# A hybrid attention and convolution layer on one core: the stores of precomputed input forms on ScalarE's queue, attention blocks rounded in place, and another order of copies for a paired gate

## The chip, the core and the metric

The kernel runs on one core of a Trainium2 chip. The metric is the device time of one execution in microseconds; the median of three runs before the change is 1038.19 us (1036.29 to 1043.42). TensorE is called PE in the profile, VectorE DVE, ScalarE ACT, GpSimd POOL and SyncE SP.

## The reference

256 tokens of width 2048 go through one mixer layer. All is float32.

```python
h = rmsnorm(x, pre_norm_g)
proj = h @ w_in      # q_a, c_kv, k_rope, z_mla, c_in, b_gate, c_gate, z_conv, g_mla, g_conv
q  = rmsnorm(q_a) @ w_q_b            # 16 heads, 128 plain + 64 rotary channels
kv = rmsnorm(c_kv) @ w_kv_b          # 16 heads, key 128, value 128
attn = softmax(causal(q k' * scale)) @ v
y_mla  = (attn * silu(z_mla)) @ w_o_mla
conv   = three causal taps of c_gate * c_in
y_conv = (b_gate * conv * silu(z_conv)) @ w_o_conv
merged = sigmoid(g_mla) * y_mla + sigmoid(g_conv) * y_conv
out    = x + rmsnorm(merged @ w_out, post_norm_g)
```

## The kernel before

**Products.** TensorE multiplies in a rounded float32. For full accuracy each operand is kept as a rounded part and the rest: ScalarE copies with rounding (the function split_act, its activation at L265, tile names ending in hi, or the first half of a tile such as at_both) and VectorE subtracts (L266, lo, or the second half). A product is then three matmuls. Weights come in units of 1 MB (128 x 2048), by SP into one of three buffers named raw (L167), are split in two halves of 128 x 1024 into whi and wlo (five buffers each), and a unit is 24 matmuls. TensorE takes its matmuls in the program's order, and so do the other engines their instructions; SP issues its loads in order too, each when its buffer is free.

**Stages.** From 0 to 52 us come the latents; then 16 heads follow until 600 us. A head has four quarters of channels of the convolution (cv, two accumulator banks, evicted by ScalarE or VectorE as cv_f, cv_w or cg, L807 to L824), the projections qn, kn, qr and vv, the scores (sc), a softmax and the values (o). Every four heads there are the attention's gates z. at_f and cv_f hold the branches' results. From 600 to 943 us the kernel forms the two output projections of the branches, and the two merge gates, in one interleaved list of units; then the last projection follows, to 1030 us.

**The interleaved list.** A branch block is the product of a branch with one column block of its weight, four units of 24 matmuls: p[0] to p[3] for the attention (tile at_both, bank sq), v[0] to v[3] for the convolution (cv_both). p0[3] is the fourth unit of p[0]. A set, s0 to s3, makes four gate tiles of 128 x 512 (a, b, c, d) by a scheme of seven products, Q1, V5, V6, V7, V3, V4, Q2, each two units of 12 matmuls, that multiply sums of weight blocks (rt, rb, rc, b; added on VectorE, L1272, or by an adding transfer of POOL, L1263) by sums of blocks of the input, the forms. They accumulate in the banks sX, sZ and sY. V5 and V3 write Z; V6, V7 and V4 write X. Copies from a bank are ScalarE's (L1307), sums VectorE's (L1310), and the sigmoid of a finished gate ScalarE's (L1314). interleave() puts a set's items in that order and behind each item the units named in its table; units are split two places ahead of their matmuls, and loads are sorted by when their buffer comes free and then by when they are needed. later(n, ...) puts an action n units on.

**The forms.** The generator make_forms makes the seven forms of the input long before, between the quarters of the first 14 heads, three steps a head. In four rounds SP loads two pieces of the input (x_area, L884), ScalarE scales them (L893), VectorE multiplies (L895), and for each of the seven forms ScalarE rounds into one of three buffers (form, L907), VectorE subtracts (L909, L911), and a step later SP stores 256 KB to a scratch tensor (far_form, L914), 28 stores. In the stage of the list SP loads each form whole (L937).

**The attention's blocks.** When four heads are done, POOL stores their at_f to a scratch tensor (far_at, L749, 512 KB), and SP loads it into a raw buffer (turned_at, L969), from which split_turned makes at_both. Four such pairs make the four blocks; the first two blocks are split inside the last quarter of the last head, the other two among the list's units. The channels' branch goes the same way (far_cv, L366).

Of the kernel before, what the change touches and what calls it, by code (L numbers as in the profile page):

```python
# [18 lines left out]
P = 128  # L19
# [63 lines left out]
def tile_layer(ctx: ExitStack, tc: tile.TileContext, xw, w0, xb, x, pos, pvec, post_g, wc, wz, wcv, wkr, wqk, wqr, wv, cwr, wsq, xf, out):  # L83
# [645 lines left out]
    def values(h, pt):  # L729
        vv = groups["v", h // HV]  # L730
        j = h % HV
        o = bank(f"o{h}", tag="o", bufs=1)
        vs = slice(j * DV, (j + 1) * DV)
        both = o[:, :].rearrange("p (i q) -> p i q", i=2)
        mm = matmul
        mm(both, vv[0][:, 0, vs], pt[:, :, :S], start=True, stop=False)
        yield
        mm(o[:, :S], vv[1][:, 0, vs], pt[:, 0, :S], start=False, stop=False)
        mm(o[:, P:S], vv[1][:, 1, vs], pt[:, 0, S:], start=False, stop=False)
        mm(both[:, :, P:], vv[0][:, 1, vs], pt[:, :, S:], start=False, stop=True)  # L740

        at = at_t[:, h // HV, :, :].rearrange("p t (i k x) -> p t i k x", i=4, k=HV)[:, :, :, j, :]
        f = temp("f")
        whole(f[:, :], o)
        nc.vector.tensor_tensor(at, f[:, :].rearrange("p (t i x) -> p t i x", t=NT, i=4), at, op=ALU.mult)
        if j == HV - 1:
            g = h // HV
            tc.keep_in_program_order(
                nc.gpsimd.dma_start(out=far_at[g][:, :], in_=at_f[:, 4 * g : 4 * g + 4, :].rearrange("p k s -> p (k s)"))  # L749
            )  # L750
# [3 lines left out]
    far_at, far_cv, far_m = (  # L754
        [dram.tile([P, NT * 512], F32, name=f"far_{n}{g}") for g in range(4)] for n in ("at", "cv", "m")
# [34 lines left out]
    def channels(h, i):  # L790

        if i == 0:
            cv_ps["now"] = [bank(f"cv{h}_{t}", tag="cv", bufs=2) for t in range(NT)]
        quarter(cv_ps["now"], take(u_head[h][i]), i)
        if h == H - 2 and i in (0, 2):
            u = u_first[i // 2]
            tc.keep_in_program_order(nc.sync.dma_start(out=early[u][:, :], in_=plan[u][0]))
        if i == 3:
            if h == H - 1:
                at_u[0][0]()  # L800
                ahead(u_first[0])
                for u in at_u[:2]:
                    u[1](True)
            channels_done(*divmod(h, 4))
# [71 lines left out]
    def make_forms():  # L876
# [4 lines left out]
        for c in range(KH // kq):  # L881
            for i in range(2):
# [4 lines left out]
                )  # L887
            yield
# [15 lines left out]
            def part(n, src, sign=1.0):  # L904
# [5 lines left out]
                else:  # L910
# [3 lines left out]
                    nc.sync.dma_start(  # L914
# [9 lines left out]
            for n, src, sign, following in todo:  # L924
                go = part(n, src, sign)
                if following:
                    tt(*following)
                yield
                go()
# [69 lines left out]
    at_u = [u for a, b in ((0, 2), (2, 3), (3, 4)) for u in turned_unit(far_at[a:b], at_b, a)]  # L999
    cv_u = [u for a, b in ((0, 2), (2, 4)) for u in turned_unit(far_cv[a:b], cv_b, a)]  # L1000
    for h in range(H):
# [92 lines left out]
        if h == H - 1:  # L1094
            pt = turn(ps_by_head.pop(h))
# [8 lines left out]
        if h == H - 1:  # L1104
            finish_all(values(h, pt))
        if at == 3:
# [116 lines left out]
    def weigh(nc_, t):  # L1223
# [3 lines left out]
        later(4, lambda: keep(("m", c, t), g))  # L1227
# [22 lines left out]
    def paired(i, n, c, combine):  # L1250
# [51 lines left out]
        def gate_tile(name):  # L1302
            return wide(f"s{name}{i}", "abcd"[("abcd".index(name) - i) % 4])
# [14 lines left out]
        def done_c():  # L1318
            copy("c", "X")
            later(1, lambda: plus("c", "Z"))  # L1320
            later(2, lambda: gate("c", 1, 1, -1.0))
# [9 lines left out]
        def done_y():  # L1331
# [6 lines left out]
            ("V5", (0, 0), (1, 0), (1, 1), "5", "Z", True, False, None),  # L1338
# [21 lines left out]
    def interleave(s, after):  # L1360
# [15 lines left out]
        "Q1": p[0][:2], "V5": at_u[2:3] + p[0][2:3] + at_u[3:] + p[0][3:],  # L1376
        "V6": p[1][:1], "V7": p[1][1:2], "V3": p[1][2:3], "Q2": p[1][3:] + p[2][:1],
# [291 lines left out]
```

## Time and profile before

| | us |
|---|---|
| median of 3 runs | 1038.19 |
| the profiled execution | 1039.11 |
| its span in the trace | 1037.3 |
| PE busy | 1011.0 |
| DVE busy | 806.2 |
| ACT busy | 591.8 |
| POOL busy | 171.8 |

The span is what the trace covers; the execution's own time has 1.8 us more. Busy times are shares of one span: they say which engine is full on average, while the rows of the waits say where an engine stood still and for whom. A row of the waits has the total, the number of waits and the longest; in the timeline a bracket behind a row gives the idle time before it and what ended it. A row of a chain or a timeline begins with its start and its length in us.

### The profile page before, as it was taken

Reading aid. Unit: us, or ns where it says so; the run is one execution under the profiler, and the core shown is the slowest. Engines: PE = TensorE matmul, PEld = TensorE weight load, DVE = VectorE, ACT = ScalarE, POOL = GpSimd, SP = SyncE. Lnnn points to the kernel's source line nnn. Section 1 sums busy time; section 2 is a strip of 40 time slices with the busy share of each in tenths; the row PEclk is TensorE's granted clock in tenths of the full one; section 3 lists DMA queues with packets and bytes.
Section 4 is the critical chain, followed back from the end, with each engine's and each line's share of the span. In section 5 each row is a group of like instructions: output and inputs, shape, how many; then the busy total and the mean of one; then the engine's idle time right before and its main releaser. Section 6 shows DMA issues by size and latency. Waiting matters only on the chain.

```text
span 1037.3 us, 13027 instructions
## 1 busy us (share of the span) xinstructions
PE 1011.0 (97%) x4552; PEld 836.9 (81%) x4552; DVE 806.2 (78%) x1103; ACT 591.8 (57%) x854; POOL 171.8 (17%) x315
## 2 busy tenths in 40 slices
PE   9999999999999999999999996999999999999997
PEld 8887888887888878778888875888788888878886
DVE  7589778767887677867787696889889779987562
ACT  7676656655665455555655463655665665565451
POOL 4520411203311222212133120000000101012000
PEclk9999999999999999999999998999999999999999
DMA  8775878668776688766688889697589979648842
GB/s 341 287 262 213 264 254 273 225 191 300 251 277 219 203 291 267 245 220 222 236 289 323 315 292 357 237 365 202 178 307 299 339 279 288 235 151 293 301 170 81
DMA packets 56674, 268.14 MB, mean 258 GB/s; under 512 B 9024, under 2 KB 13760, under 8 KB 31520
## 3 DMA queue, kind: packets, MB, share of 16 engines
q1 hardware_dynamic: 43488, 225.89, 59.9%
q0 software_dynamic: 12832, 40.23, 14.3%
q10 hardware_dynamic: 288, 1.20, 0.3%
q8 instruction: 35, 0.57, 0.2%
q14 instruction: 31, 0.25, 0.1%
HBM read 238.99 MB, written 24.12 MB: 254 GB/s over the span
## 4 chain that ended last, share of the span: by engine, by line
PE 88%; DMA 7%; DVE 3%; ACT 1%; issue 1%; SPq 0%; DVEq 0%; ACTq 0%
PE cv L88 28%; PE sq L88 16%; PE sX L88 8%; PE out L88 8%; PE z L88 8%; DMA far_form<-form 4%; PE sZ L88 4%; PE qa L88 2%; PE sY L88 2%; PE ckv L88 2%; PE vv L88 2%; PE kn L88 2%; PE qn L88 2%; DMA raw<-wsq_dram 1%; DVE wlo L266 1%; DMA x_area<-xf_dram 1%
## 5 line engine op out<-in xcount | busy, mean ns | idle before, releaser
L265 ACT ACTIVATE whi<-raw 128x1024 fp32r<-128x1024 f32 (+1 forms) x302 | 305.3, 1027 | 234.6 <-PE cv L88 89.4
L266 DVE TENSOR_TENSOR wlo<-raw,whi 128x1024 fp32r<-128x1024 f32 (+1 forms) x300 | 352.4, 1189 | 108.9 <-ACT whi L265 81.8
L88 PE MATMUL cv<-whi,x_both 128*128 128x512 f32 x1024 | 321.0, 390 | 4.7 <-ACT cv_f L811 2.9
L88 PEld LDWEIGHTS cv<-whi,x_both 128*128 128x128 f32 x1024 | 192.2, 188 | 46.1 <-ACT cv_f L811 3.7
L88 PE MATMUL cv<-wlo,x_both 128*128 128x512 f32 x512 | 199.6, 390 | 0.9 <-DVE wlo L266 0.9
L88 PEld LDWEIGHTS cv<-wlo,x_both 128*128 128x128 f32 x512 | 96.1, 188 | 20.3 <-DVE wlo L266 1.2
L266 DVE TENSOR_TENSOR slo_V<-b,shi_V 128x1024 fp32r<-128x1024 f32 x60 | 71.8, 1222 | 18.7 <-PE sq L88 12.1
L265 ACT ACTIVATE shi_V<-b 128x1024 fp32r<-128x1024 f32 x60 | 61.5, 1053 | 39.8 <-PE sq L88 22.7
L88 PE MATMUL z<-whi,x_both 128*128 128x512 f32 x256 | 79.9, 389 | 0.0
L366 POOL DMA_DIRECT2D far<-via x64 | 35.2, 557 | 227.1 <-DVE via L358 224.7
L88 PE MATMUL sq<-whi,at_both 128*128 128x512 f32 x256 | 63.4, 402 | 5.6 <-ACT whi L265 5.6
L88 PEld LDWEIGHTS sq<-whi,at_both 128*128 128x128 f32 x256 | 49.9, 195 | 16.7 <-ACT whi L265 6.0
L88 PE MATMUL sq<-whi,cv_both 128*128 128x512 f32 x256 | 60.6, 389 | 0.0
L88 PEld LDWEIGHTS sq<-whi,cv_both 128*128 128x128 f32 x256 | 48.0, 188 | 10.0
L88 PEld LDWEIGHTS z<-whi,x_both 128*128 128x128 f32 x256 | 48.1, 188 | 9.9
L88 PE MATMUL z<-wlo,x_both 128*128 128x512 f32 x128 | 49.8, 389 | 0.0
L88 PE MATMUL out<-whi,m_both 128*128 128x512 f32 x208 | 49.4, 389 | 0.0
L88 PE MATMUL sX<-shi_V,form 128*128 128x512 f32 x192 | 47.4, 389 | 0.0
L88 PEld LDWEIGHTS out<-whi,m_both 128*128 128x128 f32 x208 | 39.0, 188 | 8.1
L88 PEld LDWEIGHTS sX<-shi_V,form 128*128 128x128 f32 x192 | 36.0, 188 | 7.5
L1263 POOL DMA_DIRECT2D b<-wsq_dram x8 | 6.9, 863 | 208.6 <-DVE b L1272 95.7
L265 ACT ACTIVATE shi_Q<-b 128x1024 fp32r<-128x1024 f32 x28 | 28.8, 1052 | 22.1 <-PE sq L88 17.7
(305 smaller groups left out, 1572.7 us busy)
## 6 DMA issues: line engine op xcount, KB each, us to landing
raw<-wcv_dram SPq DMA_DIRECT2D x64, 1024.0 KB, 6.3
raw<-wsq_dram SPq DMA_DIRECT2D x48, 1024.0 KB, 6.9
b<-wsq_dram SPq DMA_DIRECT2D x26, 1024.0 KB, 5.1
raw<-wz_dram SPq DMA_DIRECT2D x16, 1024.0 KB, 4.9
raw<-wqk_dram SPq DMA_DIRECT2D x8, 1024.0 KB, 7.6
b<-wsq_dram POOLq DMA_DIRECT2D x8, 1024.0 KB, 9.2
far_form<-form SPq DMA_DIRECT2D x28, 256.0 KB, 7.5
form<-far_form SPq DMA_DIRECT2D x7, 1024.0 KB, 10.9
```

What stands on the lines that cost most here:

```text
L88: return tc.keep_in_program_order(nc.tensor.matmul(*a, **kw))
L265: a = nc.scalar.activation(hi, src, AF.Copy)
L266: b = nc.vector.tensor_tensor(lo, src, hi.bitcast(F32), op=ALU.subtract)
L366: tc.keep_in_program_order(queue.dma_start(out=f[i], in_=m))
L1263: tc.keep_in_program_order(nc.gpsimd.dma_start(out=dst[:, :], in_=wsq[n, c + b, k], accum_op=ALU.add))
```

## The change

It has four edits.

- The forms' stores are issued by ScalarE instead of SP. Loading a round's input becomes a function, bring(c): the first is called ahead of the rounds with a step of its own, the next when the last form of a round is made, so that every round's scaling falls a step later than it did.
- The attention blocks are split from at_f, where they lie, by split_branch(i): blocks 0 and 1 before the last head's pt, block 2 in its last quarter, block 3 behind its values. far_at, turned_at and their four stores and four loads are gone. The first branch unit is loaded and split before the last values.
- In s0's table all four units of p[0] stand behind Q1, and the units of p[1] move to V5, V6, V7 and Q2.
- Of gate c, which is the sum of banks Z and X, ScalarE copies Z one unit after V5, VectorE adds X right behind V7, and the sigmoid comes a unit later; before, ScalarE copied X behind V7, VectorE added Z a unit later, and the sigmoid came after two. The gate tiles' tags rotate in another order, and the weighed tiles are stored two units later instead of four.

```diff
@@ -743,16 +743,11 @@
         nc.vector.tensor_tensor(at, f[:, :].rearrange("p (t i x) -> p t i x", t=NT, i=4), at, op=ALU.mult)
-        if j == HV - 1:
-            g = h // HV
-            tc.keep_in_program_order(
-                nc.gpsimd.dma_start(out=far_at[g][:, :], in_=at_f[:, 4 * g : 4 * g + 4, :].rearrange("p k s -> p (k s)"))
-            )
...
     at_t = at_f[:, :, :].rearrange("p (v t k) s -> p v t (k s)", v=NV, t=NT)
-    far_at, far_cv, far_m = (
-        [dram.tile([P, NT * 512], F32, name=f"far_{n}{g}") for g in range(4)] for n in ("at", "cv", "m")
+    far_cv, far_m = (
+        [dram.tile([P, NT * 512], F32, name=f"far_{n}{g}") for g in range(4)] for n in ("cv", "m")
     )
@@ -797,10 +792,8 @@
             if h == H - 1:
-                at_u[0][0]()
                 ahead(u_first[0])
-                for u in at_u[:2]:
-                    u[1](True)
+                split_branch(2)
             channels_done(*divmod(h, 4))
@@ -878,13 +871,17 @@
         sums_2 = [early_pool.tile([P, kq, P], F32, name=f"form_sum{i}") for i in range(2)]
-        for c in range(KH // kq):
+        def bring(c):
             for i in range(2):
...
                 )
+
+        bring(0)
+        yield
+        for c in range(KH // kq):
             yield
@@ -911,7 +908,7 @@
                 return lambda: tc.keep_in_program_order(
-                    nc.sync.dma_start(
+                    nc.scalar.dma_start(
                         out=far_form[n][:, c * w : (c + 1) * w], in_=f[:, :, :, :].rearrange("p k j c -> p (k j c)").bitcast(F32)
@@ -925,6 +922,8 @@
                     tt(*following)
+                if n == "3" and c < KH // kq - 1:
+                    bring(c + 1)
                 yield
@@ -996,7 +995,11 @@
     at_b, cv_b = (Late(n, lambda i, n=n: both_tile(n, i)) for n in ("at", "cv"))
-    at_u = [u for a, b in ((0, 2), (2, 3), (3, 4)) for u in turned_unit(far_at[a:b], at_b, a)]
+
+    def split_branch(i):
+        for t in range(NT):
+            split_turned(at_t[:, i, t, :], at_b[i], t, True)
+
     cv_u = [u for a, b in ((0, 2), (2, 4)) for u in turned_unit(far_cv[a:b], cv_b, a)]
@@ -1092,6 +1095,8 @@
         if h == H - 1:
+            split_branch(0)
+            split_branch(1)
             pt = turn(ps_by_head.pop(h))
@@ -1102,7 +1107,11 @@
         if h == H - 1:
+            load_raw(done["raw"])
+            split_unit(done["split"])
+            done.update(raw=done["raw"] + 1, split=done["split"] + 1)
             finish_all(values(h, pt))
+            split_branch(3)
         if at == 3:
@@ -1224,7 +1233,7 @@
         nc.vector.tensor_tensor(g[:, :], sums_of[n, c][t][:, :], g[:, :], op=ALU.mult)
-        later(4, lambda: keep(("m", c, t), g))
+        later(2, lambda: keep(("m", c, t), g))
@@ -1300,7 +1309,10 @@
         def gate_tile(name):
-            return wide(f"s{name}{i}", "abcd"[("abcd".index(name) - i) % 4])
+            tags = list("acbd")
+            for _ in range(i):
+                tags = tags[3:] + tags[:3]
+            return wide(f"s{name}{i}", tags["acbd".index(name)])
@@ -1316,9 +1328,8 @@
         def done_c():
-            copy("c", "X")
-            later(1, lambda: plus("c", "Z"))
-            later(2, lambda: gate("c", 1, 1, -1.0))
+            plus("c", "X")
+            later(1, lambda: gate("c", 1, 1, -1.0))
@@ -1335,7 +1346,7 @@
             ("Q1", (0, 0), None, None, "11", "X", True, False, lambda: copy("a", "X")),
-            ("V5", (0, 0), (1, 0), (1, 1), "5", "Z", True, False, None),
+            ("V5", (0, 0), (1, 0), (1, 1), "5", "Z", True, False, lambda: later(1, lambda: copy("c", "Z"))),
             ("V6", (0, 0), (1, 2), (0, 0) if by_transfer else None, "6", "X", False, False, lambda: copy("b", "X")),
@@ -1373,8 +1384,7 @@
     interleave(s0, {
-        "Q1": p[0][:2], "V5": at_u[2:3] + p[0][2:3] + at_u[3:] + p[0][3:],
-        "V6": p[1][:1], "V7": p[1][1:2], "V3": p[1][2:3], "Q2": p[1][3:] + p[2][:1],
+        "Q1": p[0], "V5": p[1][:1], "V6": p[1][1:2], "V7": p[1][2:3], "Q2": p[1][3:] + p[2][:1],
     })
```

Three places show how the instructions move. The first is ScalarE in a round of forms, at about 375 to 387 us of the trace before; a form's number ends in its tile, whi is a weight's rounding. Before:

```order
L907 ACTIVATE form_2_3874<-form_sum_1014 128x2x128
L265 ACTIVATE whi_0_3680<-raw_3643 128x1024
L265 ACTIVATE whi_1024_3684<-raw_3643 128x1024
L265 ACTIVATE whi_0_3732<-raw_3678 128x1024
L265 ACTIVATE whi_1024_3736<-raw_3678 128x1024
L265 ACTIVATE whi_0_3798<-raw_3730 128x1024
L433 ACTIVATE half<-qr_3688 128x256
L907 ACTIVATE form_2_3913<-form_sum_1015 128x2x128
L811 ACTIVATE cv_f<-cv_0_3547,r_both 128x512
```

And now:

```order
L911 DMA far_form_653<-form_2_3629 128x512
L904 ACTIVATE form_2_3820<-form_sum_1010 128x2x128
L904 ACTIVATE form_2_3863<-form_sum_1011 128x2x128
L265 ACTIVATE whi_0_3669<-raw_3632 128x1024
L265 ACTIVATE whi_1024_3673<-raw_3632 128x1024
L265 ACTIVATE whi_0_3721<-raw_3667 128x1024
L265 ACTIVATE whi_1024_3725<-raw_3667 128x1024
L265 ACTIVATE whi_0_3787<-raw_3719 128x1024
L433 ACTIVATE half<-qr_3677 128x256
L804 ACTIVATE cv_f<-cv_0_3538,r_both 128x512
```

The rounding of the second form has moved from the row before the cv_f eviction to the start of the run of weight roundings, and the store of a form that used the same set of three buffers stands ahead of the two roundings.

The second place is SP at the transition from the heads to the list, at about 606 to 633 us; raw_5943 is p0[3] and raw_5966 p1[0] before, raw_5743 to raw_5827 are p0[0] to p0[3] now, and raw_5852 is p1[0]. Before:

```order
L1258 DMA first_rc_5787<-wsq_dram 128x2048
L1258 DMA first_rc_5788<-wsq_dram 128x2048
L167 DMA raw_5828<-wsq_dram 128x2048
L969 DMA turned_at_5852<-far_at_643 128x1024
L937 DMA form_5789<-far_form_655 128x2048
L167 DMA raw_5943<-wsq_dram 128x2048
L937 DMA form_5790<-far_form_656 128x2048
L167 DMA raw_5966<-wsq_dram 128x2048
```

And now:

```order
L167 DMA raw_5743<-wsq_dram 128x2048
L167 DMA raw_5805<-wsq_dram 128x2048
L167 DMA raw_5807<-wsq_dram 128x2048
L1267 DMA first_rb_5792<-wsq_dram 128x2048
L1267 DMA first_rb_5793<-wsq_dram 128x2048
L936 DMA form_5791<-far_form_650 128x2048
L1267 DMA first_rc_5796<-wsq_dram 128x2048
L1267 DMA first_rc_5797<-wsq_dram 128x2048
L167 DMA raw_5827<-wsq_dram 128x2048
L936 DMA form_5798<-far_form_651 128x2048
L167 DMA raw_5852<-wsq_dram 128x2048
```

The turned block has gone, the four units of p[0] stand ahead of the second form that this part loads, and p1[0] stands right behind that form (form_5798).

The third is ScalarE at the same transition, from about 595 us; whi of raw_5796 before and raw_5743 now is p0[0]. Before:

```order
L265 ACTIVATE pt<-p 128x384
L265 ACTIVATE whi_0_5687<-first_rt_5306 128x1024
L265 ACTIVATE whi_1024_5691<-first_rt_5306 128x1024
L265 ACTIVATE whi_0_5722<-first_rt_5307 128x1024
L818 ACT_TABLE_LOAD
L818 ACTIVATE cg<-cv_0_5564,r_both 128x512
L265 ACTIVATE whi_1024_5726<-first_rt_5307 128x1024
L265 ACTIVATE at_both_5730<-turned_at_5719 128x4x128 x2
L265 ACTIVATE at_both_5735<-turned_at_5719 128x4x128 x2
L433 ACTIVATE half<-o_5748 128x256
L818 ACTIVATE cg<-cv_1_5565,r_both 128x512
L265 ACTIVATE whi_0_5807<-raw_5796 128x1024
```

And now:

```order
L265 ACTIVATE at_both_5682<-at_f 128x4x128 x2
L265 ACTIVATE pt<-p 128x384
L265 ACTIVATE whi_0_5690<-first_rt_5299 128x1024
L265 ACTIVATE whi_1024_5694<-first_rt_5299 128x1024
L265 ACTIVATE whi_0_5722<-first_rt_5300 128x1024
L811 ACT_TABLE_LOAD
L811 ACTIVATE cg<-cv_0_5557,r_both 128x512
L265 ACTIVATE whi_1024_5726<-first_rt_5300 128x1024
L265 ACTIVATE at_both_5730<-at_f 128x4x128 x2
L433 ACTIVATE half<-o_5753 128x256
L811 ACTIVATE cg<-cv_1_5558,r_both 128x512
L265 ACTIVATE whi_0_5745<-raw_5743 128x1024
```

The splits of blocks 0 and 1 have moved ahead of pt (of the two rows the second is shown), that of block 2 stands where they stood, and p0[0]'s rounding stands behind the second cg in both.

## The prediction

> **What bounds the kernel now.** I read the page's busy table and clock line first, then TensorE's row of the waits, then the stretches.
>
> ```profile
> PE 1011.0 (97%) x4552; PEld 836.9 (81%) x4552; DVE 806.2 (78%) x1103; ACT 591.8 (57%) x854; POOL 171.8 (17%) x315
> PE 88%; DMA 7%; DVE 3%; ACT 1%; issue 1%; SPq 0%; DVEq 0%; ACTq 0%
> ```
> ```profile
> 300.00:400.00 100.00, 97.90 (x447) 81.13 (x446) 77.65 (x130) 56.09 (x87) 18.81 (x35) 1.00 0.73 240
> 400.00:500.00 100.00, 95.77 (x449) 79.75 (x449) 73.70 (x122) 54.13 (x90) 18.19 (x34) 1.00 0.69 235
> 500.00:600.00 100.00, 100.00 (x461) 83.43 (x461) 76.68 (x129) 54.06 (x85) 25.54 (x47) 1.00 0.84 301
> 600.00:650.00 50.00, 40.32 (x162) 31.46 (x162) 40.81 (x41) 25.62 (x32) 6.75 (x11) 0.93 0.90 321
> ```
> ```profile
> PE sq L88 <- ACT whi L265: 5.6, 1, 5.6
> PE sq L88 <- DVE wlo L266: 4.1, 4, 1.8
> PE sc L88 <- DVE kn L266: 3.0, 2, 2.5
> PE cv L88 <- ACT cv_f L811: 2.9, 2, 2.1
> PE cv L88 <- ACT cv_w L815: 1.8, 1, 1.8
> PE sZ L88 <- DVE sc L1310: 1.5, 2, 0.7
> ```
>
> The bound is TensorE: 97% busy, with the same matmuls before and after the change. From 500 to 600 us it never pauses (100.00 in the second column). So only its pauses can be won, and the six rows are nearly all of them: total us, times, longest. They fall in three groups. The head loop (kn, cv_f, cv_w) pauses 3.0 + 2.9 + 1.8 = 7.7 us. The transition at 600 to 650 us (sq) pauses 5.6 + 4.1 = 9.7 us, and there the granted clock (the number before the DMA share) is 0.93 instead of 1.00. The sets (sZ) pause 1.5 us. The change speaks to one group with each of its parts, so the ceiling is about 19 us plus what the low clock cost.
>
> **Part one: the stores of the forms go by ScalarE's queue.** The chain that sets the end passes through these stores, and the timeline shows how:
>
> ```profile
> 238.08 0.72 SPq L914 DMA_DIRECT2D far_form<-form  x1
> 248.19 0.42 ACT L907 ACTIVATE form<-form_sum 128x256 fp32r<-128x256 f32 x1 [4.78 <-DMA far_form<-form]
> 248.52 0.67 ACT L811 ACTIVATE cv_f<-cv,r_both 128x512 f32<-128x512 f32 x1
> 249.24 0.50 PE L88 MATMUL cv<-whi,x_both 128*128 128x512 f32 x1 [0.80 <-ACT cv_f L811]
> 385.03 0.42 ACT L907 ACTIVATE form<-form_sum 128x256 fp32r<-128x256 f32 x1 [6.08 <-DMA far_form<-form]
> 386.07 0.50 PE L88 MATMUL cv<-whi,x_both 128*128 128x512 f32 x1 [2.10 <-ACT cv_f L811]
> ```
> ```profile
> 238.08 10.09 DMA far_form<-form
> ```
> ```profile
> ACT form L907 <- DMA far_form<-form: 30.5, 13, 6.1
> ```
> ```profile
> far_form<-form SPq DMA_DIRECT2D x28, 256.0 KB, 7.5
> raw<-wqr_dram SPq DMA_DIRECT2D x8, 256.0 KB, 3.9
> ```
> ```profile
> ACT whi L265 <- PE cv L88: 89.4, 71, 3.6
> ```
>
> A store sits in SP's order behind weight loads, is issued at 238.08 and takes 10.09 us (7.5 is the median of 28). The form's rounding on ScalarE waits for that buffer (4.78 us), and the eviction of the channels' bank (cv_f) stands behind it; TensorE wants that bank. ScalarE waits like this 13 times for 30.5 us, but only where an eviction stands right behind does TensorE feel it: holds of 4.78 and 6.08 us cost it 0.80 and 2.10, that is, the hold less 3.98 both times.
>
> In the changed order the rounding that held the evictions has moved ahead of a run of four or five weight roundings, and no form's rounding stands in the row before an eviction any more. I therefore take all of cv_f and cv_w (2.9 + 1.8 = 4.7) as won. Of kn's two waits (3.0 in all, longest 2.5) the shorter, 3.0 - 2.5 = 0.5, has the same cause and goes too. The longer is another thing:
>
> ```profile
> 404.67 1.33 SPq L884 DMA_DIRECT2D x_area<-xf_dram  x2
> 413.40 1.71 ACT L893 ACTIVATE x_area<-x_area,pv 128x256 f32<-128x256 f32 x4 [3.26 <-DMA x_area<-xf_dram]
> 416.75 0.39 PE L88 MATMUL sc<-kn,qn_hi 128*128 128x256 f32 x1 [2.45 <-DVE kn L266]
> 168.28 0.69 ACT L815 ACTIVATE cv_w<-cv,r_both 128x512 f32<-128x512 f32 x1
> 170.68 1.71 ACT L893 ACTIVATE x_area<-x_area,pv 128x256 f32<-128x256 f32 x4 [0.32 <-DMA x_area<-xf_dram]
> ```
>
> That is the input of the forms coming late (issued 404.67, used 413.40), and its load keeps its place behind the same weight load on SP. A store's 256 KB no longer lies just ahead of it; at the 235 GB/s of that stretch these are 1.1 us, of which I take about half, 0.6, as won (from 0 to 2.45). The first scaling of the inputs now stands ahead of the second cv_w eviction, which was at 168.28 while the inputs were used at 170.68: if the inputs land at 170, the eviction ends near 171.3, where TensorE would like the bank at 170.3. I charge 1.0 (from 0 to 2). Sum of the part: 4.7 + 0.5 + 0.6 - 1.0 = 4.8.
>
> What it costs: 28 issues on ScalarE. The row of 238.08 has 0.72 for SP's issue of the same store, a weight's issue below has 0.33; 28 x 0.5 = 14 us on an engine that is idle for 43% of the span. The last row above says what lies in hand: ScalarE waits 71 times for TensorE to free a weight buffer, so all five halves are then full; each serves 12 matmuls, 2.72 us, and less the one in use and a rounding and subtraction of its own some 8 us are left. Issues of 0.5 don't reach TensorE. More serious is that sixteen of the stores now stand one to four rows ahead of the rounding that waits for that same buffer, and ScalarE stands still until they land. How long that is on this queue no row shows; the ends are 3.9, the median of SP's 256 KB loads, and the 10.09 of the chain's row. I take 6, nearer to the lower end, since no weight load is queued ahead of the store any more: held 5 us with 8 in hand, nothing reaches TensorE. The other end is a rival below.
>
> The Trainium skill, in "DMA: Bandwidth & Descriptors" under "Issuing engines are not separate DMA queues", says that transfers started by different engines all run on the same 16 DMA engines, and that issuing from several saves only issue time. By that rule the stores land no sooner than before, which is a rival below. The same page, under "Queues, rings and completion order", has each DMA engine take turns among the rows of queues, which would let a store pass a waiting megabyte. No row of this trace decides between them.
>
> **Part two: the attention blocks rounded in place, the first block early.** These rows are the transition:
>
> ```profile
> 603.63 0.69 ACT L818 ACTIVATE cg<-cv,r_both 128x512 f32<-128x512 f32 x1
> 604.22 3.89 ACT L265 ACTIVATE whi<-raw 128x1024 fp32r<-128x1024 f32 x4
> 611.16 0.73 PE L88 MATMUL sq<-wlo,at_both 128*128 128x512 f32 x2 [1.49 <-DVE wlo L266]
> 617.57 0.95 POOL L1263 DMA_DIRECT2D first_rb<-wsq_dram  x1 [0.17 <-PE sq L88]
> 620.11 0.89 POOL L1263 DMA_DIRECT2D first_rb<-wsq_dram  x1 [1.59 <-DVE slo_V L266]
> 621.94 0.33 SPq L937 DMA_DIRECT2D form<-far_form  x1
> 624.69 0.33 SPq L167 DMA_DIRECT2D raw<-wsq_dram  x1
> 637.56 2.00 ACT L265 ACTIVATE whi<-raw 128x1024 fp32r<-128x1024 f32 x2 [12.01 <-DMA raw<-wsq_dram]
> 638.67 6.51 PE L88 MATMUL sq<-whi,at_both 128*128 128x512 f32 x16 [5.61 <-ACT whi L265]
> ```
> ```profile
> 605.88 3.79 PE L88 MATMUL sq<-whi,at_both 128*128 128x512 f32 x16
> ```
>
> The weight of p0[3] (fourth unit of the first branch block) is issued at 624.69, behind three buffers that the turned blocks and two units share, is usable at 637.56, and TensorE loses 5.61. Then 16 matmuls take 6.51 us instead of the 3.79 of 605.88: 2.7 more, the low clock. With the 4.1 of wlo the transition loses 9.7 + 2.7 = 12.4.
>
> After: the turned loads (2 MB) and stores (2 MB) are gone, the raw buffers belong to weights alone, and by my working from the loads' order p0[0] to p0[3] are all there before 617. The splits themselves are the same number and shape, only from another tile, so they cost nothing new. But they stand earlier on ScalarE: four before the last pt, two inside the last quarter. Its second cg now waits for a product of VectorE that the splits delay, by my working from 603.63 to about 606.5; then 0.69 and 1.0 (a quarter of 3.89) for the first half of p0[0]'s weight make 608.2, where TensorE is ready at 605.88. Charge 2.3 (from 0 to 3.5).
>
> Next late is p1[0], the first weight behind the form whose load is in the row of 621.94. That load waits for the tail of the channels' stores as before, so p1[0] is issued at about 623; the two transfers that add (617.57 and 620.11) come some 3.7 us later, since V5 now follows four units instead of two, and share the way with it. With 12.9 us, as from the row of 624.69 to that of 637.56, it lands at 636; with one more megabyte of the adding transfers on top, some 4 us at the 321 GB/s that the stretch moves (they read, add and write), at 640. TensorE wants it after p0[0] to p0[3] and V5: 605.88 + 2.3 + 4 x 5.44 + 2 x 2.72 = 635.4 (the 16 matmuls of 605.88 take 15 steps and one matmul's 0.39, so a step is 0.2267 and a unit of 24 is 5.44). I take the middle, 638, and 1.0 for the first half's rounding, so 3.6, and 0.6 for the wlo behind it, and 0.7 for the clock. This last is a quarter of 2.7: pauses to 2.45 us kept the rate, one of 5.61 did not, and 3.6 lies nearer the lower. Left: 2.3 + 3.6 + 0.6 + 0.7 = 7.2; won: 12.4 - 7.2 = 5.2 (from 0, when p1[0] is as late as p0[3] was, to 10, when it comes in time).
>
> The Trainium skill, "TensorE: Matmul & The Clock Gate" under "Part 1: The HAM clock gate", puts the drop to half rate at an idle window of about 3.4 us. The row of 638.67 agrees that 5.61 is over it; by that page the 3.6 would cost the whole drop, a rival below.
>
> **Part three: the gate c.** V3 writes bank Z and waits twice for VectorE's sum of Z:
>
> ```profile
> 745.66 2.11 PE L88 MATMUL sZ<-shi_V,form 128*128 128x512 f32 x8 [0.73 <-DVE sc L1310]
> ```
>
> After the change ScalarE has copied Z a unit after V5, and VectorE adds X at once behind V7; V3 finds Z read long before. The sum of X must be done before V4, one set item later, and V7's own weight needs nothing of it. All 1.5 is won (from 0.5 to 1.8). The copy is the same work of ScalarE at another place, and a gate's tile comes free sooner, so the earlier store behind it delays nobody.
>
> **The sum.** 4.8 + 5.2 + 1.5 = 11.5. The profiled execution took 1039.11 us (its span 1037.3 and 1.8 around it); 1039.11 - 11.5 = 1027.6. It stands 0.92 above the median of 1038.19; scaled to that, 1026.7. I predict 1027.0.
>
> **The rivals.**
>
> *The wait only moves* (0.20). p1[0]'s weight takes the place of p0[3]'s, with the same 5.6 + 2.7 and the wlo waits: part two wins nothing. For it: two adding transfers and a form of 1 MB lie in the same few us (the stretch 600 to 650 has its DMA share at 0.90, the highest of the four). Against it: two turned loads and a store of 512 KB each have gone from these us. 1027.0 + 5.2 = 1032.2.
>
> *The weight comes in time* (0.18). Only the 2.3 of p0[0] remains, 10.1 won instead of 5.2: 1022.1. For it: p1[0] has fewer loads beside it than p0[3] had, and its buffer is free long before; against it: the form ahead of the weight on SP waits for stores whose time hasn't changed.
>
> *The low clock comes at 3.6* (0.10). The pause is as forecast, but the matmuls behind it run as the row of 638.67 has them: 2.7 instead of 0.7, 1029.0. For it: the one pause over 2.45 had it; against it: that pause was two us longer.
>
> *The stores land no sooner* (0.08). At 7.5 on either queue, ScalarE is held 6.5 at a time, still inside the 8; the inputs gain nothing, and the shorter kn wait stays: 1027.0 + 0.6 + 0.5 = 1028.1.
>
> *ScalarE is held by its own stores* (0.08). If they take the 10.09 us of the chain's row, sixteen roundings wait about 9 us each. By the two pairs of rows above TensorE pays the hold less 3.98 where an eviction is near: I count three such places (two cv_f, one cv_w, seven or eight rows behind), 3 x 5 = 15, and at four of the others the 1 us beyond the 8 in hand. 1027.0 + 19 = 1046. It decides from a landing of about 8.5 us, where a hold uses up the weights in hand. For it: 7.5 is the median on SP's queue already. Against it: part of that was queueing behind loads.
>
> **How the numbers follow.** The forecast has 0.36, the rivals 0.20, 0.18, 0.10, 0.08 and 0.08. A measurement of this kernel can tell about 1% from no change: faster by over 1% is below 1027.8, slower above 1048.6. The forecast's own range (phase one 2.5 to 7, transition 2 to 8, sets 0.5 to 1.8) runs from 1021.5 to 1033 and has a little more than half its weight below 1027.8: 0.21; with 0.18 of the weight in time, 0.07 of the low clock and the stores, and 0.02 of the moved wait, 0.48. Slower needs the held ScalarE beyond its price: 0.05. The rest, 0.47, is within 1%. The range from 1018 (the weight in time, inputs early, all bounds kind) to 1037 (the wait moved, and the stores holding ScalarE at one or two places) leaves out the worst of the last rival.
>
> **What would show it.** Right: no wait of TensorE for cv_f, cv_w or sc; stores landing in under 6 us; first sq row waiting about 2 us; one wait of 2 to 5 us near 635 on a weight of the second block, after V5. Wrong: long waits of form's rounding on ScalarE followed by waits of cv or z for whi; a wait of p0[3] on its weight as before; a granted clock of 0.93 again in the stretch; waits of V4 for the sum of X.

## The result, and the profile after

The changed kernel took 1025.71 us (median of 4 runs, 1020.92 to 1029.02) beside 1038.60 of the kernel before on the same chip: a ratio of 0.9871 with a 95% interval of 0.9845 to 0.9896. Measured again in the last batch, it was 0.9848 (0.9829 to 0.9867). The forecast was 1027.0. The profiled execution's span is 1024.7 us, 12.6 less than before.

TensorE's waits after the change, in the form of before (total us, times, longest):

```profile
PE sc L88 <- DVE kn L266: 3.3, 1, 3.3
PE cv L88 <- ACT cv_w L808: 2.7, 2, 1.4
PE sq L88 <- ACT whi L265: 2.0, 1, 2.0
```

The sets' row (sZ) has gone, as said. Of the transition's 9.7 us one wait of 2.0 is left. But the head loop, where 4.8 were to go, still pauses 3.3 + 2.7 = 6.0 after 7.7. The stretches of the changed kernel say the same (PE busy, PEld, DVE, ACT, POOL; the granted clock is the third number from the end, then the DMA share and GB/s):

```profile
300.00:400.00 100.00, 98.59 (x452) 81.95 (x451) 76.71 (x128) 55.35 (x89) 18.42 (x34) 1.00 0.71 236
400.00:500.00 100.00, 96.73 (x443) 80.73 (x442) 74.73 (x123) 55.01 (x90) 18.12 (x34) 0.97 0.70 231
600.00:650.00 50.00, 48.04 (x214) 39.36 (x213) 46.74 (x44) 31.57 (x37) 6.19 (x10) 1.00 0.81 273
```

From 600 to 650 TensorE has 48.04 busy us where it had 40.32, its matmuls are 214 instead of 162, and the clock is 1.00. From 400 to 500 the matmuls are 443, fewer than the 449 of before, and the clock is 0.97: a low clock has appeared where there was none.

What follows from the stores' new queue, on ScalarE and in the issues (median us to landing last):

```profile
ACT form L904 <- DMA far_form<-form: 41.5, 14, 5.7
```
```profile
far_form<-form ACTq DMA_DIRECT2D x28, 256.0 KB, 5.1
x_area<-xf_dram SPq DMA_DIRECT2D x8, 256.0 KB, 7.9
```

The stores land 2.4 us sooner (5.1 after 7.5), and still ScalarE waits for them longer, 41.5 us after 30.5: ScalarE now comes to the rounding that needs the buffer 3.3 us after the store's issue (median of 25), where it came 6.5 us after it before. The inputs land as late as before (7.9 after 8.0 on the page of before).

### The profile page after: what moved, and what is told of

Read it like the earlier page. It is cut to its first block, busy times and chain, and to the rows that moved or that the text cites. A ratio compares the mean times of both kernels' runs of the same rounds, so it can differ in the third digit from the quotient of the medians.

```text
span 1024.7 us, 13006 instructions
## 1 busy us (share of the span) xinstructions
PE 1008.7 (98%) x4552; PEld 838.0 (82%) x4552; DVE 805.3 (79%) x1103; ACT 591.1 (58%) x854; POOL 170.8 (17%) x311
## 4 chain that ended last, share of the span: by engine, by line
PE 88%; DMA 5%; DVE 3%; ACT 2%; issue 1%; POOL 0%; SPq 0%; ACTq 0%; DVEq 0%
PE cv L88 26%; PE sq L88 17%; PE z L88 8%; PE out L88 8%; PE sX L88 8%; PE sZ L88 4%; DMA x_area<-xf_dram 2%; PE qa L88 2%; PE vv L88 2%; PE sY L88 2%; PE ckv L88 2%; PE qn L88 2%; PE kn L88 2%; DMA far_form<-form 2%; DVE wlo L266 2%; PE sw L88 1%
## 5 line engine op out<-in xcount | busy, mean ns | idle before, releaser
L88 PE MATMUL sq<-whi,at_both 128*128 128x512 f32 x256 | 60.8, 390 | 2.0 <-ACT whi L265 2.0
L88 PEld LDWEIGHTS sq<-whi,at_both 128*128 128x128 f32 x256 | 47.9, 188 | 12.4 <-ACT whi L265 2.6
```

The costliest lines, as they stand in the source:

```text
L88: return tc.keep_in_program_order(nc.tensor.matmul(*a, **kw))
```

## The experiments

All ratios are to the kernel before, on the same chip in the same batch.

**The first edit alone**, on the kernel before:

```diff
-        for c in range(KH // kq):
+        def bring(c):
...
+        bring(0)
+        yield
+        for c in range(KH // kq):
...
-                    nc.sync.dma_start(
+                    nc.scalar.dma_start(
                         out=far_form[n][:, c * w : (c + 1) * w], ...
...
+                if n == "3" and c < KH // kq - 1:
+                    bring(c + 1)
```

> Only the first edit: the forms' stores by ScalarE's queue and the inputs' scaling a step later. Theory 1 (the pauses only change their place): the kernel's own trace shows 3.3 us for kn and 2.7 for cv_w where before had 7.7 in all, and the one of 3.3 is followed by a low clock, so this part alone gains 0 to 2 us: 1036.5 to 1039. Theory 2 (the terms of the prediction hold, and the rest is interplay): 4.8 us gained, near 1034. Either way cv_f is gone from TensorE's waits; theory 1 wants cv_w and one kn of over 2 us among them.

Measured: 1036.92 us, ratio 0.9983 (0.9959 to 1.0006). No difference that can be told from none. TensorE's waits:

```profile
PE cv L88 <- ACT cv_w L815: 5.0, 2, 3.4
PE sc L88 <- DVE kn L266: 1.9, 1, 1.9
```

cv_f has gone from the waits, as both theories said; cv_w has grown from 1.8 to 5.0 and one kn of 1.9 stays: 6.9 after 7.7. That is theory 1 in the time and in cv_w; the kn of over 2 us that it wanted came out at 1.9.

**The second edit alone**: blocks split in place, the first unit split before the last values, and the early table.

```diff
-    at_u = [u for a, b in ((0, 2), (2, 3), (3, 4)) for u in turned_unit(far_at[a:b], at_b, a)]
+    def split_branch(i):
+        for t in range(NT):
+            split_turned(at_t[:, i, t, :], at_b[i], t, True)
...
-        "Q1": p[0][:2], "V5": at_u[2:3] + p[0][2:3] + at_u[3:] + p[0][3:],
-        "V6": p[1][:1], "V7": p[1][1:2], "V3": p[1][2:3], "Q2": p[1][3:] + p[2][:1],
+        "Q1": p[0], "V5": p[1][:1], "V6": p[1][1:2], "V7": p[1][2:3], "Q2": p[1][3:] + p[2][:1],
```

> Only the second edit: attention blocks split in place and the first block's four units behind Q1. Theory 1: 10.4 us gained, near 1028.2, with one wait of about 2 us for the first whi of the first block, no wait for raw after it, and a granted clock of 1.00 from 600 to 650. Theory 2: 5.2 gained, 1033.4, with a wait of about 3.6 us near 635 on the weight of the second block.

Measured: 1026.66 us, 0.9897 (0.9865 to 0.9928): 10.7 us on 1039.8. The same 2.0 us for the first block's whi is the only wait of sq, and the clock from 600 to 650 is 1.00:

```profile
PE sq L88 <- ACT whi L265: 2.0, 1, 2.0
```
```profile
600.00:650.00 50.00, 48.04 (x213) 39.38 (x212) 48.21 (x48) 32.85 (x37) 6.17 (x10) 1.00 0.81 271
```

Theory 1 again; the wait of 3.6 us near 635 isn't there. The head loop gives nothing to this gain: in the trace, which is of the slowest of the six executions (1031.76), TensorE waits 5.1 there for kn, 2.3 for cv_w and 1.5 for cv_f.

**The third edit alone**:

```diff
-            copy("c", "X")
-            later(1, lambda: plus("c", "Z"))
-            later(2, lambda: gate("c", 1, 1, -1.0))
+            plus("c", "X")
+            later(1, lambda: gate("c", 1, 1, -1.0))
```

> Only the third edit: ScalarE copies Z, VectorE adds X at once. Both theories: TensorE's two waits for sc (1.5 us in all) go and nothing takes their place, 1037.1; a rival, that the sum of X is late for V4 or that the copy delays a weight, would show a new wait for sX or shi and leave 1038.6.

Measured: 1036.89 us, 0.9971 (0.9947 to 0.9994). The trace has no sZ wait and no new one for sX or shi. The interval holds the 1.5 us that the trace gives.

The three ratios multiplied are 0.9983 x 0.9897 x 0.9971 = 0.9852, and the whole change had 0.9871 and 0.9848: within the noise the edits add up, and the second has most of it.

**The stores back on SP**, all else as changed:

```diff
-                    nc.scalar.dma_start(
+                    nc.sync.dma_start(
                         out=far_form[n][:, c * w : (c + 1) * w], ...
```

> The changed kernel with the forms' stores back on SP; the later scaling and all else stay. If ScalarE's queue itself gives the gain of the head loop (stores landing at a median of 5.1 us instead of 7.5), the long holds of form's rounding and TensorE's waits for cv_f come back and it takes 2 to 5 us more than the changed kernel, 1028 to 1031. If the later step gives it, the time is that of the changed kernel, 1026, or 1 to 2 us better since ScalarE is not held by its own stores.

Measured: 1033.60 us, 0.9941 (0.9915 to 0.9967), some 7 us slower than the changed kernel's ratio. The size is above what was expected, and the place is another: cv_f does not come back, cv_w has a wait of 2.9 and kn waits 4.6.

```profile
PE sc L88 <- DVE kn L266: 4.6, 2, 3.9
PE cv L88 <- ACT cv_w L808: 2.9, 1, 2.9
```
```profile
303.15 0.42 ACT L904 ACTIVATE form<-x_area 128x256 fp32r<-128x256 f32 x1 [6.94 <-DMA far_form<-form]
303.47 0.67 ACT L808 ACTIVATE cv_w<-cv,r_both 128x512 f32<-128x512 f32 x1
304.20 0.50 PE L88 MATMUL cv<-whi,x_both 128*128 128x512 f32 x1 [2.94 <-ACT cv_w L808]
```

The long hold of a form's rounding is back, as the first theory said, but ahead of a cv_w eviction near 304 instead of cv_f: a hold of 6.94 us costs TensorE 2.94, again the hold less 4. So the new step alone takes the roundings away from cv_f, on SP's queue too, and leaves one in front of cv_w. Without any of part one the two other edits would give 0.9897 x 0.9971 = 0.9868, if they add up (no run has just these two); with the step on SP's queue it is 0.9941, so there the step would cost more than it gives. The trace can't show where all of that goes: it is of the fastest of nine executions (1029.0).

**The later step taken back**, the stores on ScalarE:

```diff
-        def bring(c):
+        for c in range(KH // kq):
...
-        bring(0)
-        yield
-        for c in range(KH // kq):
...
-                if n == "3" and c < KH // kq - 1:
-                    bring(c + 1)
```

> The changed kernel with only the later step taken back: the inputs are loaded and scaled at the old steps, the stores stay on ScalarE's queue. Theory 1 (the later step costs what the queue wins): the cv_w wait near 170 and the late input before kn near 412 shrink or go, together 1.5 to 6 us with the low clock behind the latter: 1020 to 1024. Theory 2 (the later step is what took the rounding away from the evictions): waits for cv_f near 248 and 384 come back, 1026 to 1030.

Measured: 1022.54 us, 0.9844 (0.9811 to 0.9876). The time falls where theory 1 said, but its interval overlaps those of the changed kernel (0.9871, 0.9848), so a gain isn't shown; its trace has kn at 0.5 us and no cv_f, and cv_w at 3.7. Of the two waits that theory 1 named only the one before kn shrank; the one for cv_w near 170 grew from 1.3 to 2.5, since the scaling stands right ahead of that eviction without the step too:

```profile
169.37 0.91 ACT L886 ACTIVATE x_area<-x_area,pv 128x256 f32<-128x256 f32 x2 [3.22 <-DMA x_area<-xf_dram]
170.18 0.67 ACT L808 ACTIVATE cv_w<-cv,r_both 128x512 f32<-128x512 f32 x1
```

The step hardly moves the scaling in time: the last three rounds are scaled from 169, 287 and 412 us without it and from 170, 285 and 412 with it. Theory 2 falls, since cv_f does not return without the step: on ScalarE's queue the step isn't needed for that.

**The inputs' loads a step sooner**:

```diff
-                if n == "3" and c < KH // kq - 1:
+                if n == "7" and c < KH // kq - 1:
                     bring(c + 1)
```

> The changed kernel with each load of the inputs after the first issued one step sooner, when the sixth form of a round is made; scaling stays. Theory 1 (TensorE's 3.3 us for kn and the low clock are the input's late landing): the kn wait near 412 and the cv_w wait near 305 go, 3.4 + 2.5 + 1.6 = 7 us at most, 1019 to 1022. Rival (the loads only take turns with the weights, so that another weight comes late, or the scaling's place on ScalarE is what holds): 1025 to 1027.

Measured: 1029.48 us, 0.9908 (0.9872 to 0.9944). A miss for theory 1. Of the waits:

```profile
PE sc L88 <- DVE kn L266: 4.0, 2, 3.0
PE cv L88 <- ACT cv_w L808: 3.3, 1, 3.3
```
```profile
ACT x_area L890 <- DMA x_area<-xf_dram: 15.3, 6, 5.6
```

The wait before kn near 412 shrank to 1.0, but another of 3.0 arose near 280, and ScalarE waits 15.3 us for inputs after 6.2. The loads came sooner by 2 to 9 us in the trace, but the scaling did not stay: it starts at 167, 280 and 403 instead of 170, 285 and 412, so ScalarE comes to it before the inputs are there, and near 280 it now stands ahead of kn. Why the order came out so this run doesn't settle.

**The inputs' loads on GpSimd**, at the same step of the program as in the changed kernel:

```diff
         def bring(c):
             for i in range(2):
                 tc.keep_in_program_order(
-                    nc.sync.dma_start(
+                    nc.gpsimd.dma_start(
```

> The changed kernel with the inputs' loads issued by GpSimd at the same step, so that they do not stand behind the weight loads in SP's order. Theory 1 (the place in SP's order makes them late): they land in about 5 us instead of 7.9, and the kn wait near 412 falls by over 1.5 us with its low clock, 1020 to 1023. Rival (all queues share the engines, and the time from issue to landing stays): 1025 to 1027 with the same wait.

Measured: 1017.10 us, 0.9792 (0.9759 to 0.9826): faster than theory 1 said, and faster than the changed kernel with intervals apart. The stretches of the head loop:

```profile
100.00:200.00 100.00, 100.00 (x472) 83.90 (x471) 78.20 (x138) 61.63 (x106) 21.32 (x39) 1.00 0.75 259
200.00:300.00 100.00, 100.00 (x466) 83.68 (x465) 79.40 (x132) 52.97 (x84) 26.60 (x49) 1.00 0.78 260
300.00:400.00 100.00, 100.00 (x459) 83.47 (x458) 77.86 (x130) 59.19 (x95) 18.99 (x35) 1.00 0.70 231
400.00:500.00 100.00, 99.33 (x467) 83.03 (x466) 79.30 (x132) 57.31 (x95) 18.37 (x34) 1.00 0.69 240
```
```profile
ACT x_area L890 <- DMA x_area<-xf_dram: 1.2, 2, 0.8
```
```profile
x_area<-xf_dram POOLq DMA_DIRECT2D x8, 256.0 KB, 6.9
```

```profile
189.62 0.90 ACT L890 ACTIVATE x_area<-x_area,pv 128x256 f32<-128x256 f32 x2
304.66 1.71 ACT L890 ACTIVATE x_area<-x_area,pv 128x256 f32<-128x256 f32 x4 [0.40 <-DMA x_area<-xf_dram]
431.69 1.70 ACT L890 ACTIVATE x_area<-x_area,pv 128x256 f32<-128x256 f32 x4
```

TensorE is full for 300 us. But not for the reason that theory 1 gave: the transfers are hardly shorter (6.9 after 7.9). What moved is the place. In the order that came out with GpSimd's loads the last three rounds are scaled at 190, 305 and 432, where the changed kernel has them at 170, 285 and 412, and GpSimd issues these loads at 184, 296 and 425 instead of 161, 278 and 404: the same step of the program, but 18 to 23 us later in time. At its new places the scaling no longer stands ahead of the evictions and kn that TensorE was waiting for, and the data is there (1.2 us of waiting after 6.2). How much of the gain is the queue, and how much these 19 to 20 us, this run can't tell, since both changed at once.

**GpSimd's loads without the later step**:

```diff
-        def bring(c):
+        for c in range(KH // kq):
             for i in range(2):
...
-                    nc.sync.dma_start(
+                    nc.gpsimd.dma_start(
...
-        bring(0)
-        yield
-        for c in range(KH // kq):
...
-                if n == "3" and c < KH // kq - 1:
-                    bring(c + 1)
```

> The changed kernel with the inputs' loads by GpSimd and the later step taken back; the forms' stores stay on ScalarE. Theory (the head loop's remaining pauses are all the input's landing, and the later step only moved the scaling): as good as with the later step, 1015 to 1019, no TensorE wait over 1 us between 100 and 600. Rival (the later step is what makes the loads by GpSimd work): cv_w or kn waits come back, 1020 to 1024.

Measured: 1017.71 us, 0.9785 (0.9768 to 0.9802), two waits for cv_w between 100 and 600, 0.8 us together. As the theory said: with the loads on GpSimd the step is worth nothing. It isn't the step that moved the scaling, though: the last three rounds are scaled from 189, 303 and 430 us here too. Beside the run without the step and with the inputs on SP (0.9844) the loads on GpSimd give some 6 us, with intervals apart.

**The same with the stores on SP**:

```diff
-                    nc.scalar.dma_start(
+                    nc.sync.dma_start(
                         out=far_form[n][:, c * w : (c + 1) * w], ...
```

> The same with the forms' stores on SP as before, so that of the first edit nothing is left but the inputs on GpSimd. If ScalarE's queue matters by itself (stores of 5.1 us instead of 7.5 that no longer hold the rounding in front of evictions), cv_f or cv_w waits of 1 to 2 us each come back and it takes 1020 to 1025. If the inputs' landing was all, 1016 to 1019.

Measured: 1020.99 us, 0.9817 (0.9799 to 0.9835). At the lower end of the first forecast: a cv_f wait of 1.0 and a kn of 0.8 come back, and the medians differ by some 3 us (the profiled execution, 1018.75, is the shortest of the five). The two intervals touch, so the queue's own worth here is near 3 us and not settled closer.

```profile
PE cv L88 <- ACT cv_f L804: 1.0, 1, 1.0
PE sc L88 <- DVE kn L266: 0.8, 1, 0.8
```

**The old table with the blocks in place**:

```diff
-        "Q1": p[0], "V5": p[1][:1], "V6": p[1][1:2], "V7": p[1][2:3], "Q2": p[1][3:] + p[2][:1],
+        "Q1": p[0][:2], "V5": p[0][2:], "V6": p[1][:1], "V7": p[1][1:2], "V3": p[1][2:3], "Q2": p[1][3:] + p[2][:1],
```

> The changed kernel with the first branch block's units back in the old places (two behind Q1, two behind V5), blocks still split in place. Theory 1 (the in-place blocks free the raw buffers, and the early order removes what VectorE's two sums delay): p0[3]'s weight comes in time, but the wlo wait of p0[2] behind the two sums returns, 1.8 + 0.4, so 1027 to 1029. Rival (the early order is what lets the weight come in time): the 5.6 us wait and the low clock return too, 1034 or more. Second rival (the order does nothing): 1026.

Measured: 1034.44 us, 0.9960 (0.9938 to 0.9982): 0.0089 of 1038, some 9 us, worse than the changed kernel. The rival was right, in the wait and in the clock (0.90 from 600 to 650). In TensorE's waits and the chain:

```profile
PE sq L88 <- ACT whi L265: 8.3, 2, 6.4
```
```profile
620.11 16.45 DMA raw<-wsq_dram
636.66 1.06 ACT whi L265
```

p0[3]'s weight is again the one behind the form on SP (issued at 620.11 after the form at 619.73), takes 16.45 us beside the two adding transfers, and is needed at 631.4, while p1[0]'s in the same place is needed at 635.4.

**The early table with turned blocks**, on the kernel before:

```diff
-        "Q1": p[0][:2], "V5": at_u[2:3] + p[0][2:3] + at_u[3:] + p[0][3:],
-        "V6": p[1][:1], "V7": p[1][1:2], "V3": p[1][2:3], "Q2": p[1][3:] + p[2][:1],
+        "Q1": p[0][:2] + at_u[2:3] + p[0][2:3] + at_u[3:] + p[0][3:], "V5": p[1][:1],
+        "V6": p[1][1:2], "V7": p[1][2:3], "Q2": p[1][3:] + p[2][:1],
```

> The kernel before with only the table of s0 changed: all four units of the first block behind Q1, the turned blocks still stored and loaded. Theory (the early order can't work without the in-place blocks): the last turned block landed at 624.4 in the trace before and is needed at 622 now, and the raw buffers are shared with it, so a wait of 3 to 6 us stands at the fourth unit, 1035 to 1041. Rival (the order is the gain, the in-place rounding nothing): 1028 to 1031.

Measured: 1047.84 us, 1.0076 (1.0050 to 1.0103). Slower, as neither forecast had it; the wait is one unit earlier than I named:

```profile
PE sq L88 <- ACT whi L265: 18.3, 1, 18.3
```
```profile
612.69 24.22 DMA raw<-wsq_dram
```

The third unit's weight is issued at 612.69 behind the two pairs of sums and a form, and takes 24.22 us; in the changed kernel it is loaded before them. Either half of the second edit without the other loses nearly all its gain: the order without in place is at 1.0076, both together at 0.9897, and the changed kernel without the order at 0.9960 beside 0.9871 with it.

**The changed kernel again**:

> The changed kernel once more, on the same chip as the three above. 1024 to 1028; the pause before kn near 412 is 2.5 to 4 us again if its cause is the inputs' load (issued near 404, landing near 413), and it moves by a microsecond with the landing.

Measured: 1024.12 us, 0.9848 (0.9829 to 0.9867). The time is as expected; the kn pause, 2.3 us at 415, is just below its forecast. For cv_w there is one pause, 3.4 us at 173, and none near 306: the pauses before kn and near 170 come back with other sizes, the one near 306 doesn't.

## Why the prediction was right in time, and where its steps failed

The time was right, in part by luck: two of its three terms were wrong, in opposite directions.

*Part one, 4.8 us.* Failed: it is worth between nothing and 4 us (0.9959 to 1.0006 alone). In the trace the head loop's pauses fall by 1.7 (7.7 to 6.0) instead of 4.8. The 4.7 and the 0.5 came: the evictions were freed of the roundings at the old places, no cv_f is in the waits, and of kn's two waits one is left. Two other terms were wrong, the charge for the scaling and the late input. For the scaling ahead of cv_w I charged 1.0; the changed kernel waits 2.7 for cv_w, at two places. Its chain shows them:

```profile
161.28 8.31 DMA x_area<-xf_dram
169.62 0.51 ACT x_area L890
170.12 0.58 ACT cv_w L808
285.42 9.94 DMA far_form<-form
305.92 0.70 ACT cv_w L808
```

The first, at 170, is the predicted one, 1.3 us. It goes with the stores on ScalarE: with the inputs on SP, all six traces that have the stores there wait 1.3 to 3.4 us for cv_w between 169 and 173, with the later step or without it, and none of the five with the stores on SP does. The second, at 306, is the rival of ScalarE held by its own stores, at one of the three places: by the chain, a store that took 9.94 us made work of ScalarE and VectorE late that a cv_w eviction 10 us after its landing still waited for. In the second trace of the changed kernel that store lands at 295 too, and TensorE, which had lost more at 173, does not wait there. And the late input was taken to win 0.6; it lost:

```profile
404.70 8.80 DMA x_area<-xf_dram
```
```profile
416.08 0.58 PE L88 MATMUL sc<-kn,qn_hi 128*128 128x256 f32 x1 [3.27 <-DVE kn L266]
418.81 1.05 PE L88 MATMUL cv<-whi,x_both 128*128 128x512 f32 x2
423.12 0.63 PE L88 MATMUL cv<-whi,x_both 128*128 128x512 f32 x2
```

The row is the second of two loads; the first is issued at 404.21, in the trace of before at 404.67, since the program has them at the same step in both. The rounding of kn that stands behind the scaling comes 0.7 us earlier than before (414.34 after 415.01), but TensorE, which lost less ahead of it, comes 1.5 us earlier (412.43 after 413.91 for the last matmul before the pause) and so waits 3.27 instead of 2.45. The matmuls behind run slowly: two at 418.81 take 1.05, two at 423.12 take 0.63. From the sc matmul behind the pause to the same cv matmul further on pass 6.35 us (416.08 to 422.43), before 3.59 (416.75 to 420.34). These 2.8 us of low clock, which part one put at nothing, are more than the 1.7 that the pauses gave. A gain ahead of a fixed load is given back there. In the runs with GpSimd's loads, whose scaling stands elsewhere, the head loop has no pauses to speak of.

*Part two, 5.2 us.* What is won, 12.4, and the first charge were right; the charge for p1[0] was not, and so the size was half. Predicted 2.3 for p0[0] against 2.0 measured. The 3.6 for p1[0], its wlo and its clock did not come: the rival that the weight comes in time was the true one (10.1 us; the second edit alone gained 10.7, and the waits fell from 9.7 to 2.0 with the 2.7 of the clock). I had p1[0] there at 638 and it landed at 631.7: 2.2 us of that are its issue, 2.0 its transfer, and 2.0 what I added for the adding transfers. The issue hangs on the form's load ahead of it, which waits for the channels' stores. These stores' times to landing, with the median in the middle, before and after:

```profile
DMA to landing us min/median/max: 5.0/7.4/8.0
```
```profile
DMA to landing us min/median/max: 2.0/2.4/3.7
```

I took them to land as before. The first is issued at 614.46 instead of 610.29, the last at 618.3 instead of 616.85, where before it had stood behind a wait of 2.74 for the attention block's store. That store and the turned block's load are no longer there, the weights of p0[0] to p0[2] have been moved by then, and that of p0[3] lands at 618; the channels' stores land in 2.4 us. Which of these did it no run separates. So the chain is shorter:

```profile
620.38 0.33 SPq L936 DMA_DIRECT2D form<-far_form  x1
620.80 0.85 SPq L167 DMA_DIRECT2D raw<-wsq_dram  x2
631.70 2.01 ACT L265 ACTIVATE whi<-raw 128x1024 fp32r<-128x1024 f32 x2 [3.14 <-DMA raw<-wsq_dram]
635.45 3.79 PE L88 MATMUL sq<-whi,at_both 128*128 128x512 f32 x16
```

p1[0] is issued at 620.80 instead of 623, is split from 631.70 on, and TensorE takes it without a pause at 635.45; 635.4 was the predicted need. The time that its transfer took, 10.9 us, was also below my 12.9, although the two adding transfers were issued beside it, at 621.46 and 623.65, as the prediction had them: the 4 us for their megabyte, of which the forecast took half, did not come. In-place blocks and the early order need each other, which the prediction didn't say: the two experiments on the table show that neither alone does it.

*Part three, 1.5 us.* Right: the sZ row is gone and nothing took its place.

*The rivals.* The stores landed sooner, 5.1 us by the median, between the 6 that I took and the 3.9 of the row, and at 7.1 with only the queue put back: the Trainium skill's rule in "DMA: Bandwidth & Descriptors", "Issuing engines are not separate DMA queues", doesn't hold for the time to landing here, while the turns among queues that the same page has under "Queues, rings and completion order" would fit it. That is not shown: no run here looked at the packets. The rival of the low clock had no pause of 3.6 near 635 to follow, but at 416 a pause of 3.27 lost the rate.

The sum came right by luck: an overestimate of some 3 us met an underestimate of some 5.

## What to carry to other kernels

Cost a reordering by what the freed place exposes: when an eviction no longer waits for one thing, look for the next load whose issue is fixed by something else, since a gain ahead of it is given back there. Before pricing a wait as it was, ask which traffic the change takes out of the microseconds in which the transfer runs. And look where the waiting instruction stands before asking how fast its data comes: moving the eight input loads off SP, which shifted their scaling by some 20 us, took 6 to 8 us off the changed kernel (0.9792 beside 0.9871 and 0.9848), though they land only 1 us faster. What the 28 stores' new queue is worth depends on that place too: some 7 us with the inputs on SP and the later step, some 3 us with the inputs on GpSimd.

## What the runs showed of the hardware that was not expected

The clock falls after pauses of very different length. A pause of 1.96 us before the same 16 matmuls left the rate in the changed kernel and lost it in the run with the old table:

```profile
608.06 3.98 PE L88 MATMUL sq<-whi,at_both 128*128 128x512 f32 x16 [1.96 <-ACT whi L265]
```
```profile
607.42 5.54 PE L88 MATMUL sq<-whi,at_both 128*128 128x512 f32 x16 [1.96 <-ACT whi L265]
```

That is 1.6 us more for one pause of the same length. Of the ten traces with this pause (1.96 or 1.97 us) five kept the rate and five lost it, the fastest kernel's among the latter. The rule of the Trainium skill's "TensorE: Matmul & The Clock Gate", "Part 1: The HAM clock gate", of a window of about 3.4 us that runs free of the kernel fits a result that depends on when the pause falls, though it speaks of an idle window and these pauses are shorter; no run here shows the window. So a pause of 2 us costs 2 or about 3.5, and a rate lost near 416 us (after 3.27) is a part of the 4.8 that part one didn't bring.
